# Ordering the last 48 rows of a sum of reciprocals by one list, in place of the last 24

## The chip, the cores and the metric

The kernel runs on one core of a Trainium2 chip. The metric is the device time of one execution in microseconds. The kernel before takes 169.41 us (median of the 6 runs that stood beside the changed kernel, 169.25 to 169.90). Ratios in this document are the mean time of one kernel's fast runs over the mean of the other's in the same rounds, so they are not quite the ratio of the medians quoted beside them.

## The reference

```python
x = np.abs(np.random.randn(32, 512, 1024)).astype(np.float32) + 1e-6
return np.sum(1.0 / x, axis=-1).astype(np.float32)
```

This is 67 MB in and 64 KB out. Each of the 128 partitions has 128 rows of 1024 numbers.

## The kernel before

A row has two halves, a and b. As 1/a + 1/b = (a + b) / (ab), half as many reciprocals are needed. GpSimd (or VectorE) makes the product ab, ScalarE makes 1/ab of it by Ln and Exp, and VectorE multiplies and sums. For some rows TensorE makes a + b in PSUM first (matmuls with an identity), and VectorE then has half the width to go over. Rows come into a ring of 40. Most rows are handled in a loop, in pairs. The last 24 follow a list, in which each letter is an operation and each number a row:

```python
    R = 40
    A, B, C = (2, 0, 0), (2, 2, 0), (2, 2, 1)
    LOADS = [[A, B, A, B], [A, B, A, C]] * 5 + [[A, B], [A, C]] * 3
    LAST = 104
    LAST_LOADS = [2] * 1 + [4] * 1 + [2] * 5 + [1] * 8
    ORDER = """
        P104 P105 L104+ P107 B106 E104+ V106 P109 B108 L106+ T104 P110+ S108
        ...
        S123 P124 E122+ T119 D125 S125 L124 T122 L125 P126 T121 E124 S126 E125
        T123 L126 T124 W127 E126 T125 X127 T126
    """
    # P product on GpSimd, D on VectorE; B copies b into PSUM for V, a product on VectorE;
    # S adds the halves on TensorE; L Ln, E Exp; T product and sum on VectorE;
    # W, X: Ln, and Exp with the sum, of a whole row. A plus sign: this row and the next.

    for n in LAST_LOADS:                       # all loads of the last rows, then the list
        xt = ring[:, c0 % R : c0 % R + n, :]
        keep(nc.sync.dma_start(out=xt, in_=x_v[:, c0 : c0 + n, :]))
        c0 += n
    ...
    nc.sync.dma_start(out=out_v, in_=sums)
```

All transfers are issued by SyncE, and their landings are counted in eight counters that take turns: transfer 1 uses the first, transfer 9 the first again. In the trace of the kernel before, each issue from the ninth load on comes after the landing of the load eight before, from the 19th load on 0.06 or 0.07 us after it. The kernel before has 31 loads and the output.

Of the kernel before, what the change touches and what calls it, by code (L numbers as in the profile page):

```python
# [11 lines left out]
def kernel(  # L12
# [15 lines left out]
    nc = tc.nc  # L28
# [4 lines left out]
    F = 128  # L33

    R = 40
# [3 lines left out]


    A, B, C = (2, 0, 0), (2, 2, 0), (2, 2, 1)
    LOADS = [[A, B, A, B], [A, B, A, C]] * 5 + [[A, B], [A, C]] * 3






    LAST = 104
    LAST_LOADS = [2] * 1 + [4] * 1 + [2] * 5 + [1] * 8  # L50
    ORDER = """
        P104 P105 L104+ P107 B106 E104+ V106 P109 B108 L106+ T104 P110+ S108
        E106+ V108 T105 L108+ S109 T106 L110+ P112+ T107 E108+ S112 E110 T108
        L112+ P114+ T109 S113 T110 E111 E112+ T111 L114+ P116 S116 T113 E114+
        T112 P117 L116 T114 P119 B118 L117 E116 S118 V118 E117 P120 T115 L118+
        P121 S119 T116 E118+ T117 P122 L120+ S122 T118 E120+ D123 L122+ T120
        S123 P124 E122+ T119 D125 S125 L124 T122 L125 P126 T121 E124 S126 E125
        T123 L126 T124 W127 E126 T125 X127 T126
    """

    Ln = mybir.ActivationFunctionType.Ln
# [4 lines left out]
    x_v = x.flatten_outer_dims().rearrange("(p f) d -> p f d", p=P)  # L66
# [24 lines left out]
    ring = opool.tile([P, R, D], f32)  # L91
# [3 lines left out]
    keep = tc.keep_in_program_order  # L95

    def add(bank, *halves):
        for k, half in enumerate(halves):
            i = nc.tensor.matmul(  # L99
                bank,  # L100
                lhsT=ident,
                rhs=half,
                start=k == 0,
                stop=k == len(halves) - 1,  # L104
            )
            keep(i)  # L106

    def sum_row(c, row, fac, out=None):
        i = nc.vector.tensor_tensor_reduce(  # L109
            out=row if out is None else out,  # L110
            in0=row,
            in1=fac,
            scale=S,
            scalar=0.0,
            op0=mult,
            op1=plus,
            accum_out=sums[:, c : c + 1],
        )
        keep(i)

    def sum_rows(c, xc, pr, sm, rc):
        m, e = xc.shape[1], len(sm)
        for j in range(e, m):
            row = xc[:, j, :].rearrange("p (h e) -> p h e", h=2)  # L124
            sum_row(  # L125
                c + j,  # L126
                row,
                rc[j - e].unsqueeze(1).to_broadcast([P, 2, H]),
                pr[:, e : e + 2, :] if j == e and e + 1 < m else None,
            )  # L130
        for j in reversed(range(e)):
            sum_row(c + j, pr[:, j, :], sm[j])

    waiting = None
    c0 = 0
    for chunks in LOADS:
        n = sum(m for m, _, _ in chunks)
        xt = ring[:, c0 % R : c0 % R + n, :]
# [3 lines left out]
        for m, e, v in chunks:  # L142
            pr = ppool.tile([P, m, H], f32, tag="ps" if e else "pr")
            for j in range(v):
# [3 lines left out]
                    out=pr[:, j, :], in0=xt[:, q + j, :H], in1=b, op=mult  # L148
# [6 lines left out]
        for (m, e, v), pr in zip(chunks, made):  # L155
            xc = xt[:, q : q + m, :]
            if v < m:
                i = nc.gpsimd.tensor_tensor(  # L158
                    out=pr[:, v:, :], in0=xc[:, v:, :H], in1=xc[:, v:, H:], op=mult
# [22 lines left out]
        c0 += n  # L182
    assert c0 == LAST, c0

    c0 = LAST
    for n in LAST_LOADS:
        xt = ring[:, c0 % R : c0 % R + n, :]
        keep(nc.sync.dma_start(out=xt, in_=x_v[:, c0 : c0 + n, :]))
        c0 += n
    assert c0 == F, c0  # L190
    sum_rows(*waiting)

    prs, rs, ss, bs = {}, {}, {}, {}
    order = ORDER.split()
# [3 lines left out]
    def pair(c):  # L198
        k = (c - LAST) // 2
        if k not in prs:  # L200
            pr = ppool.tile([P, 2, H], f32, tag=("pr", "ps")[k % 2])
            prs[k] = pr
        return prs[k]

    for op in order:
        kind, c, n = op[0], int(op[1:].rstrip("+")), 1 + op.endswith("+")
        j = (c - LAST) % 2
        rows = ring[:, c % R : c % R + n, :]
        a, b = rows[:, :, :H], rows[:, :, H:]
        pr = None if kind in "WX" else pair(c)[:, j : j + n, :]  # L210
        if kind == "P":
            keep(nc.gpsimd.tensor_tensor(out=pr, in0=a, in1=b, op=mult))  # L212
        elif kind == "D":
            keep(nc.vector.tensor_tensor(out=pr, in0=a, in1=b, op=mult))  # L214
        elif kind == "B":
            bb = bpool.tile([P, H], f32, tag="b")
            add(bb, b[:, 0, :])
            bs[c] = bb
        elif kind == "V":
            keep(  # L220
                nc.vector.tensor_tensor(  # L221
                    out=pr[:, 0, :], in0=a[:, 0, :], in1=bs[c], op=mult
                )
            )
        elif kind == "S":
            s = spool.tile([P, H], f32, tag="s")
            add(s, a[:, 0, :], b[:, 0, :])
            ss[c] = s
        elif kind == "L":
            keep(nc.scalar.activation(out=pr, in_=pr, func=Ln, scale=S))  # L230
        elif kind == "E":
            r = pr
            if c not in added:
                r = rpool.tile([P, n, H], f32, tag="rc")
                rs.update({c + l: r[:, l, :] for l in range(n)})
            keep(nc.scalar.activation(out=r, in_=pr, func=Exp, scale=-1.0))  # L236
            if n == 2:
                dead.add((c - LAST) // 2)
        elif kind == "T" and c in added:
            sum_row(c, pr[:, 0, :], ss[c])  # L240
        elif kind == "T":
            row = rows[:, 0, :].rearrange("p (h e) -> p h e", h=2)
            k = (c - LAST) // 2
            to = prs[k] if k in dead else None
            dead.discard(k)
            sum_row(c, row, rs[c].unsqueeze(1).to_broadcast([P, 2, H]), to)
        elif kind == "W":
            keep(nc.scalar.activation(out=rows, in_=rows, func=Ln))  # L248
        elif kind == "X":
            keep(  # L250
                nc.scalar.activation(
                    out=rows,
                    in_=rows,
                    func=Exp,
                    scale=-1.0,
                    accum_out=sums[:, c : c + 1],
                )
            )

    nc.sync.dma_start(out=out_v, in_=sums)  # L260

# [29 lines left out]
```

## Time and profile before

| Quantity | Before | View |
|---|---|---|
| traced span | 167.6 us | page |
| input queue, share of the span | 94.8% | DMA queues |
| row 127 lands | 161.8 us | issue and time to landing |
| ScalarE's last sum is read | 165.19 us | ScalarE's timeline |
| output issued, landed | 165.21, 166.8 us | the same views |

The table is read from the end: the stream of loads lasts until 161.8, the work on the last row 3.4 us more, then the output, and then some 0.8 us until the last instruction. The traced run took 169.71 us, 0.3 more than the median. The lines themselves stand in the prediction.

### The profile page before, as it was taken

How to read it: one execution, taken by the hardware profiler on the slowest of the kernel's cores; microseconds unless marked ns; L12 is line 12 of the kernel's file. 1: busy time of each engine (PE TensorE's matmuls, PEld its weight loads, DVE VectorE, ACT ScalarE, POOL GpSimd, SP SyncE). 2: the span in 40 equal slices, each digit the busy share in tenths (PEclk: the TensorE clock that was granted, in tenths of full speed). 3: DMA queues.
4: the chain of work that ended last, by engine and by line, in shares of the span. 5: the costliest groups of instructions: out<-in, count | busy, mean ns of one | idle time of the engine just before them, and what ended most of it. 6: DMA issues, size and time to landing. Idle time of an engine off the chain costs nothing.

```text
span 167.6 us, 1286 instructions
## 1 busy us (share of the span) xinstructions
PE 130.3 (78%) x274; PEld 50.2 (30%) x274; DVE 122.6 (73%) x267; ACT 134.8 (80%) x137; POOL 135.7 (81%) x73
## 2 busy tenths in 40 slices
PE   0007899796987959878699869977999995998990
PEld 0003343232233313322333224322343422433430
DVE  0000777758977578884788877778989899998994
ACT  3002888979789688868879788799999998999994
POOL 1007999699895999949998898999999997999630
PEclk9999999999999999999789999999999999999999
DMA  6999999999999999999999999999999999999910
GB/s 203 422 446 430 446 422 399 461 399 446 414 409 454 407 446 422 442 424 446 430 430 422 414 418 434 424 434 434 420 426 413 436 416 416 422 413 410 409 71 18
DMA packets 4615, 67.25 MB, mean 401 GB/s; under 512 B 512, under 2 KB 640, under 8 KB 1664
## 3 DMA queue, kind: packets, MB, share of 16 engines
q1 hardware_dynamic: 4608, 67.18, 94.8%
q8 instruction: 2, 0.03, 0.1%
q14 instruction: 5, 0.04, 0.1%
HBM read 67.11 MB, written 0.07 MB: 401 GB/s over the span
## 4 chain that ended last, share of the span: by engine, by line
DMA 72%; POOL 11%; ACT 9%; DVE 2%; issue 2%; PE 1%; ACTq 1%; SPq 0%; POOLq 0%
DMA ring<-in_x_dram 72%; POOL pr L158 11%; ACT pr L230 3%; ACT pr L169 2%; ACT pr L236 2%; DVE ring L109 1%; ACT r L236 1%; PE bb L99 1%; ACT r L174 1%; ACT ring L248 1%; ACTq L286 1%; DVE pr L109 0%; DVE pr L221 0%; SPq L139 0%; ACT pr L179 0%
## 5 line engine op out<-in xcount | busy, mean ns | idle before, releaser
L99 PE MATMUL s<-ring,ident 128*128 128x512 f32 x252 | 120.3, 617 | 30.7 <-DMA ring<-in_x_dram 15.2
L158 POOL TENSOR_TENSOR pr<-ring 128x1024 f32<-128x1024 f32 (+1 forms) x52 | 112.8, 2209 | 21.8 <-DMA ring<-in_x_dram 21.8
L99 PEld LDWEIGHTS s<-ring,ident 128*128 128x128 f32 x252 | 46.3, 193 | 101.8 <-issue 61.9
L169 ACT ACTIVATE pr<-pr 128x1024 f32<-128x1024 f32 x52 | 54.7, 1053 | 27.3 <-POOL pr L158 27.3
L109 DVE CUSTOM_DVE_ANT_1 pr<-ring,r 128x1024 f32<-128x1024 f32 x30 | 36.6, 1221 | 41.5 <-ACT r L174 40.8
L109 DVE CUSTOM_DVE_ANT_1 ring<-ring,r 128x1024 f32<-128x1024 f32 x34 | 41.3, 1217 | 0.0
L109 DVE CUSTOM_DVE_ANT_0 pr<-pr,s 128x512 f32<-128x512 f32 x63 | 40.9, 683 | 0.0
L179 ACT ACTIVATE pr<-pr 128x1024 f32<-128x1024 f32 x26 | 27.5, 1057 | 0.8
L174 ACT ACTIVATE r<-pr 128x1024 f32<-128x1024 f32 x26 | 26.7, 1028 | 0.8
L212 POOL TENSOR_TENSOR pr<-ring 128x512 f32<-128x512 f32 (+1 forms) x15 | 22.3, 1504 | 3.9 <-DMA ring<-in_x_dram 3.6
L230 ACT ACTIVATE pr<-pr 128x1024 f32<-128x1024 f32 (+1 forms) x14 | 12.5, 900 | 0.5 <-DVE pr L221 0.5
L109 DVE DVE_READ_ACCUMULATOR2_ANT sums<- 128x1 f32 x127 | 10.5, 83 | 0.0
L99 PE MATMUL b<-ring,ident 128*128 128x512 f32 x16 | 9.0, 646 | 0.3 <-DMA ring<-in_x_dram 0.2
L236 ACT ACTIVATE r<-pr 128x1024 f32<-128x1024 f32 (+1 forms) x8 | 6.4, 806 | 0.1
L236 ACT ACTIVATE pr<-pr 128x1024 f32<-128x1024 f32 (+1 forms) x7 | 6.0, 863 | 0.1
L147 DVE TENSOR_TENSOR pr<-ring,b 128x512 f32<-128x512 f32 x8 | 5.5, 684 | 0.7 <-PE b L99 0.7
L99 PE MATMUL bb<-ring,ident 128*128 128x512 f32 x6 | 3.4, 644 | 2.2 <-DMA ring<-in_x_dram 1.5
L99 PEld LDWEIGHTS b<-ring,ident 128*128 128x128 f32 x16 | 3.0, 207 | 6.0 <-DMA ring<-in_x_dram 4.1
L221 DVE TENSOR_TENSOR pr<-ring,bb 128x512 f32<-128x512 f32 x3 | 2.1, 688 | 0.4 <-PE bb L99 0.2
L99 PEld LDWEIGHTS bb<-ring,ident 128*128 128x128 f32 x6 | 0.9, 188 | 4.7 <-DMA ring<-in_x_dram 3.1
L70 ACT ACT_TABLE_LOAD x1 | 1.3, 1283 | 0.7 <-PEq L275 0.7
L214 DVE TENSOR_TENSOR pr<-ring 128x512 f32<-128x512 f32 x2 | 1.4, 686 | 0.0
(9 smaller groups left out, 3.2 us busy)
## 6 DMA issues: line engine op xcount, KB each, us to landing
ring<-in_x_dram SPq DMA_DIRECT2D x10, 4096.0 KB, 37.8
ring<-in_x_dram SPq DMA_DIRECT2D x7, 2048.0 KB, 37.0
ring<-in_x_dram SPq DMA_DIRECT2D x6, 1024.0 KB, 30.7
ring<-in_x_dram SPq DMA_DIRECT2D x8, 512.0 KB, 14.4
out_dram<-sums SPq DMA_DIRECT2D x1, 64.0 KB, 1.6
```

Of the source, the lines that this page charges most:

```text
L99: i = nc.tensor.matmul(bank, lhsT=ident, rhs=half, start=k == 0, stop=k == len(halves) - 1,)
L109: i = nc.vector.tensor_tensor_reduce(out=row if out is None else out, in0=row, in1=fac, scale=S, scalar=0.0, op0=mult, op1=plus, accum_out ...
L147: i = nc.vector.tensor_tensor(out=pr[:, j, :], in0=xt[:, q + j, :H], in1=b, op=mult)
L158: i = nc.gpsimd.tensor_tensor(out=pr[:, v:, :], in0=xc[:, v:, :H], in1=xc[:, v:, H:], op=mult)
L169: keep(nc.scalar.activation(out=pr, in_=pr, func=Ln, scale=S))
L174: nc.scalar.activation(out=r, in_=pr[:, e:, :], func=Exp, scale=-1.0)
L179: keep(nc.scalar.activation(out=r, in_=r, func=Exp, scale=-1.0))
L212: keep(nc.gpsimd.tensor_tensor(out=pr, in0=a, in1=b, op=mult))
L221: nc.vector.tensor_tensor(out=pr[:, 0, :], in0=a[:, 0, :], in1=bs[c], op=mult)
L230: keep(nc.scalar.activation(out=pr, in_=pr, func=Ln, scale=S))
L236: keep(nc.scalar.activation(out=r, in_=pr, func=Exp, scale=-1.0))
L248: keep(nc.scalar.activation(out=rows, in_=rows, func=Ln))
```

## The change

The intent is to order more of the end by hand, so that the last rows' products, Lns and sums come just in time. The list now covers rows 80 to 127. As the ring holds 40 rows, the loads of the last rows can't all be issued ahead of the list any more; each is placed in front of the first operation after which its place in the ring is free.

```diff
-    LOADS = [[A, B, A, B], [A, B, A, C]] * 5 + [[A, B], [A, C]] * 3
+    LOADS = [[A, B, A, B], [A, B, A, C]] * 5
-    LAST = 104
-    LAST_LOADS = [2] * 1 + [4] * 1 + [2] * 5 + [1] * 8
+    LAST = 80
+    LAST_LOADS = [4] * 7 + [2] * 4 + [1] * 12
     ORDER = """
-    (24 rows)
+        P80+ B82 S86 P83 L80+ S87 P84+ E80+ V82 L82+ T80 P86+ L84 T81 B90 E82+
+        ...
+        S123 T121 L124 E123 D125 E124 T122 S124 L125 W126 T123 D127 S127 E125
+        T124 L127 T125 E127 X126 T127
     """
...
+    def load(c0, below):
+        while LAST_LOADS and c0 + LAST_LOADS[0] - R <= below:
+            n = LAST_LOADS.pop(0)
+            ...
+        return c0
...
-    for op in order:
+    for at, op in enumerate(order):
+        c0 = load(c0, min(int(o[1:].rstrip("+")) for o in order[at:]))
```

It has 33 loads and the output, two more than before.

More of the change, by code (lines that the diff above doesn't have):

```diff
@@ L41 @@
     A, B, C = (2, 0, 0), (2, 2, 0), (2, 2, 1)
-    LOADS = [[A, B, A, B], [A, B, A, C]] * 5 + [[A, B], [A, C]] * 3
-    LAST = 104
-    LAST_LOADS = [2] * 1 + [4] * 1 + [2] * 5 + [1] * 8
+    LOADS = [[A, B, A, B], [A, B, A, C]] * 5
+    LAST = 80
+    LAST_LOADS = [4] * 7 + [2] * 4 + [1] * 12
     ORDER = """
-        P104 P105 L104+ P107 B106 E104+ V106 P109 B108 L106+ T104 P110+ S108
-        E106+ V108 T105 L108+ S109 T106 L110+ P112+ T107 E108+ S112 E110 T108
-        L112+ P114+ T109 S113 T110 E111 E112+ T111 L114+ P116 S116 T113 E114+
-        T112 P117 L116 T114 P119 B118 L117 E116 S118 V118 E117 P120 T115 L118+
-        P121 S119 T116 E118+ T117 P122 L120+ S122 T118 E120+ D123 L122+ T120
-        S123 P124 E122+ T119 D125 S125 L124 T122 L125 P126 T121 E124 S126 E125
-        T123 L126 T124 W127 E126 T125 X127 T126
+        P80+ B82 S86 P83 L80+ S87 P84+ E80+ V82 L82+ T80 P86+ L84 T81 B90 E82+
+        V90 L85 P88+ T82 L86+ B91 S90 T83 E86+ E85 V91 E84 T85 P92 L88+ T86
+        E88+ P93 T84 S91 L90+ P94+ T87 L92+ T88 S94 E90+ T89 P96+ E92+ T90
+        L94+ T91 S95 T93 P99 L96+ T92 S96 E94+ P98 E96 T94 E97 P101 B100 T95
+        L98+ S101 V100 P102+ L101 T97 E98+ S102 T96 L100 T98 L102+ T99 E100
+        P105 B104 E102 E101 S103 V104 P106+ E103 T101 L104+ T100 B108 E104+
+        T102 S106 P109 L106+ V108 T103 L108+ P110+ T104 S107 E106+ T105 E108+
+        S110 P112+ T106 L110+ T107 T108 S111 E110+ L112+ T109 P115 B114 E112+
+        T110 P116 S115 V114 T111 L114+ P117 T112 S114 E114+ P118 T113 L116+
+        S118 P119 T114 E116+ T115 P120 L118+ T117 S119 E118+ P121 T116 S120
+        L120 T119 P122 L121 T118 E120 S121 E121 D123 L122 T120 L123 D124 E122
+        S123 T121 L124 E123 D125 E124 T122 S124 L125 W126 T123 D127 S127 E125
+        T124 L127 T125 E127 X126 T127
     """
@@ L183 @@
     assert c0 == LAST, c0
-    c0 = LAST
-    for n in LAST_LOADS:
-        xt = ring[:, c0 % R : c0 % R + n, :]
-        keep(nc.sync.dma_start(out=xt, in_=x_v[:, c0 : c0 + n, :]))
-        c0 += n
-    assert c0 == F, c0
+    def load(c0, below):
+        while LAST_LOADS and c0 + LAST_LOADS[0] - R <= below:
+            n = LAST_LOADS.pop(0)
+            xt = ring[:, c0 % R : c0 % R + n, :]
+            keep(nc.sync.dma_start(out=xt, in_=x_v[:, c0 : c0 + n, :]))
+            c0 += n
+        return c0
     sum_rows(*waiting)
@@ L258 @@
             )
+    assert c0 == F, c0
     nc.sync.dma_start(out=out_v, in_=sums)
```

## The prediction

> **What bounds the kernel now.** I read the page's slices and queues first, then the rate in three stretches, then single loads from issue to landing, then ScalarE's timeline at the end. Of the page:
>
> ```profile
> DMA  6999999999999999999999999999999999999910
> ...
> q1 hardware_dynamic: 4608, 67.18, 94.8%
> ```
>
> The digits are DMA's busy tenths in 40 slices of the span: full in every slice but the first and the last two. One queue brings the 67.1 MB of input for 94.8% of the 167.6 us. So the kernel is a stream of loads with a short tail behind it, and only the stream's rate or the tail can be shortened. The rate by stretch (the last two columns are DMA share and GB/s; the stretches hold loads of four, two and one row):
>
> ```profile
> 102.40:131.90 29.50, 26.84 (x60) 10.71 (x60) 26.30 (x58) 27.71 (x28) 28.99 (x14) 1.00 1.01 427
> 139.30:151.70 12.40, 11.07 (x24) 4.30 (x24) 12.03 (x27) 11.92 (x14) 11.99 (x7) 1.00 1.01 419
> ```
>
> After the length come the busy us of PE, its weight loads, VectorE, ScalarE and GpSimd. All but the weight loads are 89 to 98% busy in both, yet the DMA share is 1.0: the engines keep pace and the stream never starves. The last load of one row, its issue in the timeline and its time to landing in the DMA view:
>
> ```profile
> 151.76 0.33 SPq L188 DMA_DIRECT2D ring<-in_x_dram  x1
> ```
>
> ```profile
> ring<-in_x_dram SPq DMA_DIRECT2D x1, 512.0 KB, 10.1
> ```
>
> Row 127 lands at 151.76 + 10.1 = 161.86. Read the same way, the last load of eight rows lands at 64.81 + 37.6 = 102.41, the sixth of four at 94.84 + 37.0 = 131.84, the two-row loads from 139.28 (104.48 + 34.8) to 151.73 (127.03 + 24.7). This gives 29.43 / 6 = 4.91 us for four rows, 12.45 / 5 = 2.49 for two, and 10.13 / 8 = 1.27 for one. The last issue, 151.76, comes just after a landing at 151.73, that of the load eight before it, as most late issues do; no row of the ring holds it.
>
> ScalarE towards that landing (a row's halves a and b are multiplied, ScalarE makes 1/ab of it by Ln and Exp, VectorE multiplies this with a + b and sums; PE adds the halves of some rows, and the last row of all is inverted whole, by ScalarE alone):
>
> ```profile
> 153.68 1.06 ACT L230 ACTIVATE pr<-pr 128x1024 f32<-128x1024 f32 x1 [0.15 <-DVE pr L221]
> 154.77 1.06 ACT L236 ACTIVATE pr<-pr 128x1024 f32<-128x1024 f32 x1
> 155.73 1.05 ACT L230 ACTIVATE pr<-pr 128x1024 f32<-128x1024 f32 x1
> ...
> 159.83 1.24 ACT L230 ACTIVATE pr<-pr 128x512 f32<-128x512 f32 x2
> 160.97 0.58 ACT L236 ACTIVATE r<-pr 128x512 f32<-128x512 f32 x1
> 161.49 0.61 ACT L236 ACTIVATE pr<-pr 128x512 f32<-128x512 f32 x1
> 162.05 0.63 ACT L230 ACTIVATE pr<-pr 128x512 f32<-128x512 f32 x1
> 162.59 1.04 ACT L248 ACTIVATE ring<-ring 128x1024 f32<-128x1024 f32 x1
> 163.53 0.61 ACT L236 ACTIVATE pr<-pr 128x512 f32<-128x512 f32 x1
> 164.05 1.04 ACT L251 ACTIVATE ring<-ring 128x1024 f32<-128x1024 f32 x1
> 165.00 0.19 ACT L251 ACTIVATION_READ_ACCUMULATOR ring<-ring 128x1 f32 x1
> ```
>
> From the Ln of rows 118 and 119 at 153.68 it never idles until 165.19, when the last row's sum is read and the output goes out; 2.4 us later the span ends. The whole-row Ln of row 127 (L248) starts 0.7 us after its data: ScalarE's backlog, not the landing, sets the end, but by less than 1 us.
>
> [...] Half-megabyte loads here, queued behind one another, cost 1.27 us a row against 4.91 / 4 = 1.23: only 3% less[...]. [...] two half-row Lns of 624 ns against one pair of 1052 differ by 196 ns.
>
> **The change part by part.**
>
> *Loads.* The 48 rows came in six loads of four, one of two, one of four, five of two, eight of one; now seven of four, four of two, twelve of one. From 102.41: 7 x 4.91 brings row 107 at 136.78, 4 x 2.49 row 115 at 146.74, 12 x 1.27 row 127 at 162.0. That is 0.1 us later than 161.86, the price of four more rows alone. Rows 116 to 119 come a little earlier one by one: row 119 at about 151.8 as before, 118 at 150.55.
>
> *When loads are issued.* They are now placed inside the list, each only after the work on the row 40 places before it. Row 127 needs row 87. By the rates below rows 80 to 87, landed at 112.2, are summed by about 126, and the rule of eight loads in flight allows the last issue only at about 151.9. There are some 25 us of slack, so the stream goes on unbroken.
>
> *Work by engine, last 48 rows.* Counted in both lists (the loop's 24 rows included): GpSimd loses two pair products of 2.38 and gains one single of 1.29, -3.5 us. VectorE gains two products from the ring and one from PSUM, 3 x 0.6 = +1.8 in start-to-start steps. PE gains one copy of a half, 0.86. ScalarE trades three pair Lns for six single and four pair Exps for eight single: seven times 0.15 to 0.2 us of overhead, +1.0 to 1.4. No engine was behind the stream by much, and each had waits in those 60 us, so all of this lies beside the loads except what falls into the last 10 us.
>
> *The tail.* In the listing above a pair's Ln to its own Exp takes 1.09 us start to start, a pair's Exp 0.96, a single Ln 0.57, a single Exp 0.52 into PSUM or 0.56 in place, the whole-row Ln 0.94, the last Exp with its read 1.14. Before, from 153.68: 3 x 2.05 + 3 x 0.57 + 0.52 + 0.56 + 0.52 + 0.94 + 1.14 = 11.54, against 11.51 seen. After, from the Ln of 118 and 119: 2.05 + seven single Lns 3.99 + five Exps in place 2.80 + two into PSUM 1.04 + 0.08 because the Exp of 127 follows its own Ln at once + 0.94 + 1.14 = 12.04. Splitting the pairs 120/121 and 122/123 costs this half microsecond. The start comes earlier: row 118's product starts at 150.6 on GpSimd, 119's ends at 150.6 + 2 x 1.29 = 153.2, where before 118 went over PE and VectorE to 153.6; ScalarE should be done with rows 116/117 at 153.4. So 153.4 + 12.0 = 165.4 to 165.5, against 165.19.
>
> *The floor under it.* Row 127 now goes by VectorE's product: 162.0 + 0.05 + 0.69 + 0.03, then Ln 0.65, Exp 0.56 and row 126's last Exp 1.14, to 165.1. The backlog still ends last, by about 0.3.
>
> Sum: +0.2 to +0.3 at the end of ScalarE's work, the output as before. I take +0.2: 169.43 + 0.2 = 169.6 us.
>
> **Rivals.**
>
> *A faster tail.* Half-width work on row 127 in place of a whole-row Ln could drain the backlog. Speaking for it is the 0.7 us in which row 127 waits for ScalarE; against it the sum above, and the floor of 165.1, which leaves 0.1 us: 169.3. Even a tail that ended with the last landing would save only 165.19 - 161.86 = 3.3 us, 2.0%.
>
> *The stream starves.* A load stuck behind a late sum or product would leave DMA idle, and each idle us would add itself to the time. The slack of 25 us speaks against it. A hole of 2 us would make 171.6.
>
> *The in-order queues trip over the new order.* PE has three buffers for sums and one for copies, and the Exps of rows not added on PE two; a list that asks for one too early holds the whole engine. Before, PE waits for VectorE in this way (5.2 us between 127 and 165) at no cost. If it happened late, in the last ten rows, 0.5 to 1 us would be lost: 170.1 to 170.4. The change orders the list over all 48 rows, so I expect no more of it than before.
>
> *Smaller loads cost more than seen*, 1.35 a row in place of 1.27: +1 us, 170.5. The eight single loads before show nothing of it.
>
> **Range and chances.** The two ends I can work out, floor and backlog, lie 0.3 us apart, and a mis-stepped buffer costs under 1 us: 169.2 to 170.2. Two per cent is 3.4 us; faster would need more than the whole tail, slower a hole in the stream. Faster 0.01, within 2% 0.97, slower 0.02.
>
> **What would show it right or wrong.** DMA at 9 in slices 2 to 38; row 127 landing at 161.9 to 162.1; the last issue at about 151.9; ScalarE without idle from about 153.4 to 165.4 and first among the pieces of the chain's end. Wrong would be: a gap in the DMA row, a landing after 162.5, a wait of ScalarE or VectorE of over 0.5 us in the last 10 us, or an end of ScalarE's work before 165.0.

Cut from it are general figures for the ceiling of the data rate, for the size of transfers and for the cost of a ScalarE operation, which no trace here shows. The forecast's sum rests on none of them: it is worked out from the times in its listings and stays 169.43 + 0.2 = 169.6 us. That no order of loads could win much in the stream rested on the ceiling alone; measured are 427 GB/s with a DMA share of 1.0. Its eight loads in flight are what the trace shows by the waits described under "The kernel before".

## The result

The changed kernel takes 169.95 us (median of 6, 169.63 to 170.06) against 169.41: ratio 1.0026, 95% interval 1.0011 to 1.0041. Executions over 1.5% slower than the fastest of the same kernel are left out of the means. That is the same within 2%, and inside the predicted range. Its page:

```profile
DMA  5999999999999999999999999999999999999900
...
q1 hardware_dynamic: 4896, 67.18, 94.2%
q14 instruction: 6, 0.05, 0.1%
```

The stream is as unbroken as before. The last of these lines counts fetches of instructions within the span: six packets of 8 KB each, one more than before. The one more starts at 168.02, 0.67 us after SyncE's 80th recorded instruction; SyncE has 79 in the kernel before, and there a fetch starts at 168.64, after the span. It matters later. The stretches of four-row and two-row loads:

```profile
102.40:131.90 29.50, 24.01 (x52) 9.24 (x53) 27.16 (x57) 27.61 (x31) 28.61 (x16) 1.00 1.01 428
139.30:146.70 7.40, 7.40 (x19) 3.33 (x19) 7.40 (x18) 7.33 (x9) 7.06 (x5) 1.00 1.01 414
```

The DMA share is 1.0 in both, at 428 GB/s in the first, as before. ScalarE's timeline at the end:

```profile
153.22 1.04 ACT L240 ACTIVATE pr<-pr 128x1024 f32<-128x1024 f32 x1
154.30 1.06 ACT L246 ACTIVATE pr<-pr 128x1024 f32<-128x1024 f32 x1
155.26 1.13 ACT L240 ACTIVATE pr<-pr 128x512 f32<-128x512 f32 x2
156.30 1.13 ACT L246 ACTIVATE pr<-pr 128x512 f32<-128x512 f32 x2
...
161.93 0.57 ACT L246 ACTIVATE r<-pr 128x512 f32<-128x512 f32 x1
162.71 0.63 ACT L240 ACTIVATE pr<-pr 128x512 f32<-128x512 f32 x1 [0.21 <-DVE pr L224]
...
164.85 0.19 ACT L261 ACTIVATION_READ_ACCUMULATOR ring<-ring 128x1 f32 x1
```

Two single Lns start 155.26, and what follows them starts 156.30: 0.52 us each. At 162.71 ScalarE waits 0.21 us for the product of row 127: it has no backlog left. It is done at 165.04, earlier than before. The chain of waits says the same (start, length, what):

```profile
151.78 10.10 DMA ring<-in_x_dram
...
161.98 0.70 DVE pr L224
...
162.71 0.64 ACT pr L240
...
163.37 0.63 ACT pr L246
```

Row 127's load, issued at 151.78, lands at 161.88; then its product, its Ln, its Exp. The landing sets the end, by the path that the prediction called the floor.

So the work ends 0.15 us earlier, and the output lands at 166.6 in place of 166.8, yet the span is 168.2 in place of 167.6. The loss lies after the output's landing. SyncE's instructions of the kernel's exit from that landing on, before and then after (count, shortest/median/longest in ns, first and last start; the count of three before includes the check that saw the landing, which stands outside the five after):

```profile
L286 SPq EVENT_SEMAPHORE  x3: 17/17/28, 166.8 to 167.5; - x3
L286 SPq DRAIN  x3: 7/7/7, 166.8 to 167.2; - x3
```

```profile
L297 SPq EVENT_SEMAPHORE  x5: 17/28/28, 166.7 to 168.1; - x5
L297 SPq DRAIN  x3: 7/7/129, 166.9 to 167.7; - x3
```

Three checks more follow the landing, and one of the drains, the second, takes 129 ns and not 7; it starts at 167.35, 0.42 us after the first, where before there are 0.06 between them. In parts, from the instruction records (us):

| | landing seen to first drain | to second drain | to the end of the span | sum |
|---|---|---|---|---|
| before | 0.07 | 0.06 | 0.69 | 0.82 |
| after | 0.27 | 0.42 | 0.82 | 1.51 |

The exit costs 0.69 us more. The prediction had it "as before".

### The profile page after: what moved, and what is told of

The parts are those of the page before. It is cut to its first block, busy times and chain, and to the rows that moved or that the text cites. A ratio compares the mean times of both kernels' runs of the same rounds, so it can differ in the third digit from the quotient of the medians.

```text
span 168.2 us, 1302 instructions
## 1 busy us (share of the span) xinstructions
PE 129.8 (77%) x276; PEld 50.2 (30%) x276; DVE 123.8 (74%) x270; ACT 134.4 (80%) x144; POOL 132.3 (79%) x72
## 4 chain that ended last, share of the span: by engine, by line
DMA 67%; ACT 10%; POOL 7%; PE 5%; issue 4%; DVE 4%; SPq 1%; ACTq 1%; POOLq 0%; DVEq 0%
DMA ring<-in_x_dram 67%; POOL pr L164 7%; PE s L105 4%; ACT pr L240 3%; ACT r L246 2%; ACT pr L175 2%; ACT pr L246 2%; SPq L145 1%; DVE ring L115 1%; DVE pr L115 1%; ACT r L180 1%; ACTq L297 1%; PE bb L105 1%; DVE pr L224 0%; DVE pr L231 0%
## 5 line engine op out<-in xcount | busy, mean ns | idle before, releaser
L164 POOL TENSOR_TENSOR pr<-ring 128x1024 f32<-128x1024 f32 (+1 forms) x40 | 88.0, 2232 | 21.7 <-DMA ring<-in_x_dram 21.7
L175 ACT ACTIVATE pr<-pr 128x1024 f32<-128x1024 f32 x40 | 42.2, 1055 | 27.1 <-POOL pr L164 27.1
L222 POOL TENSOR_TENSOR pr<-ring 128x512 f32<-128x512 f32 (+1 forms) x26 | 43.6, 1702 | 2.4 <-DMA ring<-in_x_dram 1.3
L240 ACT ACTIVATE pr<-pr 128x1024 f32<-128x1024 f32 (+1 forms) x29 | 25.0, 883 | 1.2 <-DVE pr L231 0.7
L185 ACT ACTIVATE pr<-pr 128x1024 f32<-128x1024 f32 x20 | 21.2, 1058 | 0.6
L180 ACT ACTIVATE r<-pr 128x1024 f32<-128x1024 f32 x20 | 20.6, 1028 | 0.6
L246 ACT ACTIVATE r<-pr 128x1024 f32<-128x1024 f32 (+1 forms) x15 | 12.6, 843 | 0.2
L246 ACT ACTIVATE pr<-pr 128x512 f32<-128x512 f32 (+1 forms) x16 | 12.4, 805 | 0.2
L105 PE MATMUL bb<-ring,ident 128*128 128x512 f32 x14 | 7.4, 610 | 1.1 <-DVE pr L231 0.9
L105 PE MATMUL b<-ring,ident 128*128 128x512 f32 x10 | 5.6, 645 | 0.1
L231 DVE TENSOR_TENSOR pr<-ring,bb 128x512 f32<-128x512 f32 x7 | 4.8, 684 | 0.5 <-PE bb L105 0.5
```

The source lines that it names most:

```text
L105: i = nc.tensor.matmul(bank, lhsT=ident, rhs=half, start=k == 0, stop=k == len(halves) - 1,)
L164: i = nc.gpsimd.tensor_tensor(out=pr[:, v:, :], in0=xc[:, v:, :H], in1=xc[:, v:, H:], op=mult)
L175: keep(nc.scalar.activation(out=pr, in_=pr, func=Ln, scale=S))
L180: nc.scalar.activation(out=r, in_=pr[:, e:, :], func=Exp, scale=-1.0)
L185: keep(nc.scalar.activation(out=r, in_=r, func=Exp, scale=-1.0))
L222: keep(nc.gpsimd.tensor_tensor(out=pr, in0=a, in1=b, op=mult))
```

## The experiments

My first theory was the **place** of the output's counter. At the exit SyncE checks the eight counters in five instructions, in the same order in both traces. The output is transfer 32 before, whose counter is in the fifth check, and transfer 34 after, whose counter is in the second: three checks are left over for after the landing. The rivals were the **length** of SyncE's program (83 recorded instructions against 79) and the **tail** on ScalarE, as predicted. Tiny loads of 32 bytes, put between the eight-row loads, move the output to another counter and add nothing to the stream:

```diff
+    TINY = {9: [1], 8: [0]}                    # b_t2; six or eight entries in the others
...
+        for t in TINY.get(c0 // 8, []):        # after the loads that begin at rows 32 to 72
+            keep(nc.sync.dma_start(out=spare[:, 8*t : 8*t+8],
+                                   in_=x_v[0:1, 0, 8*t : 8*t+8]))
```

**Before, with two tiny loads** (b_t2).

> The kernel before with two loads of 32 bytes added in mid-stream, so that the output is the 34th transfer, as in the changed kernel; list and load sizes as before. Theory 1 (place): SyncE's last checks go over the eight landing counters in a fixed order, the output's counter now stands second in it and not last, so the time from the output's landing to the end of the span grows from 0.84 us to about 1.5; 169.4 becomes 170.0, ratio 1.0035. Theory 2 (length): the exit grows because SyncE's program is longer; two transfers more give the same 1.5 and 170.0. Theory 3 (the prediction's): the list's tail on ScalarE is what costs; this kernel has the list of before, so exit 0.84 and 169.4, ratio 1.000.

170.13 us, ratio 1.0029 (1.0005 to 1.0054). With the list of before, the exit is that of the changed kernel: 1.51 us from the landing seen to the end, with one drain of 121 ns. So the exit comes from the two transfers more and not from the list. The tail theory falls for this part; place and length are still both possible.

**Before, with eight tiny loads** (b_t8).

> The kernel before with eight such loads, so the output is the 40th transfer and its counter is again the last one checked. Place: exit 0.84, 169.4, ratio 1.000. Length: SyncE's program is now longer than the changed kernel's, so exit 1.5 or more, 170.0, ratio 1.0035. The prediction's: 169.4.

170.52 us, ratio 1.0043 (1.0015 to 1.0071): the time that length had predicted, but not in its place. From the landing seen to the end it took 0.82, as place had said. The output, however, was issued at 165.50 though ScalarE's last sum had been read at 165.11, and SyncE waited longer for its landing:

```profile
SPq L295 <- DMA out_dram<-sums: 1.5, 1, 1.5
```

against 0.9 in the kernel before. A fetch of instructions ran at 166.14, while the output was under way; that it held up the output is not shown. (The exit here is short, and yet the time long: the stall, from 165.11 to 165.50, now stands before the output's issue.)

**Changed kernel, with six tiny loads** (a_t6).

> The changed kernel with six such loads, so its output too is the 40th transfer and its counter the last one checked. Place: exit 0.84 in place of 1.54, ScalarE's work still ends at about 165.05, so 169.3 and ratio 0.999, faster than both. Length: exit 1.5, 169.95, ratio 1.003. The prediction's: the tail is the list's, nothing changes, 169.95.

169.28 us, ratio 0.9991 (0.9955 to 1.0027), and a span of 167.3 in place of 168.2. The exit is 0.82, as place expected and length did not. But this trace has a stall too, where it does no harm. SyncE's instructions for the last load:

```profile
L205 SPq EVENT_SEMAPHORE  x1: 17/17/17, 151.6 to 151.6; - x1
L205 SPq DMA_DIRECT2D ring<-in_x_dram x1: 328/328/328, 152.0 to 152.0; - x1
```

The check passes at 151.58 and the issue starts at 152.02, 0.44 us later; such a pair is usually 0.06 apart.

**The changed kernel again** (a_again).

> The changed kernel once more, on the same chip and in the same rounds: does the exit of 1.54 us come again, and with it 169.95 (ratio 1.003)? If the exit varies from run to run (0.84 to 1.54), no theory of its cause by program is needed: then 169.3 to 170.

170.26 us, ratio 1.0036 (1.0010 to 1.0063); the exit was 1.51 again, with the stall at the same instruction. So in both runs it stands at the same place of the program. The times of one kernel scatter here more than in the first rounds, from 169.55 to 170.70.

Counting SyncE's recorded instructions gives the second theory. In all the four programs with more than 79 of them the stall comes just after the **79th**: in the exit (83 instructions, changed kernel and b_t2), before the output's issue (90, b_t8), before the last load's issue (92, a_t6). The kernel before has exactly 79. I call this place a **boundary** of the program; what happens in the hardware there is not shown. Drains on SyncE, in a stretch where it has nothing to do (3.7 to 25.0 us in the kernel before), move the program across it and leave the counters alone:

```diff
+        if c0 == 32:                           # after the fifth load is issued
+            for _ in range(4):                 # or 16
+                keep(nc.sync.drain())
```

**Before, with four drains** (b_d4).

> The kernel before with four empty instructions (drains) on SyncE after its fifth load, where SyncE has 20 us to spare. In every trace so far SyncE lost some 0.4 us right after its 79th recorded instruction: in the changed kernel (83) inside the exit, in the run with eight tiny loads before the output's issue, in the one with six in mid-stream; the kernel before has 79 in all. Boundary theory: now 83 instructions, the output's counter still checked last, so the exit grows by the boundary's part alone, 0.36 before the second drain and 0.12 after it, from 0.82 to 1.3 us; 169.4 becomes 169.9, ratio 1.003. Place alone: exit 0.82, 169.4, ratio 1.000.

170.06 us, ratio 1.0031 (1.0009 to 1.0052). The exit takes 1.31 us: 0.08 to the first drain, 0.43 to the second, 0.80 to the end.

```profile
L289 SPq DRAIN  x3: 7/7/116, 167.2 to 168.0; - x3
```

The slow drain is there with the counter in its old place: the boundary's part by itself is 1.31 - 0.82 = 0.49. (In this traced run ScalarE also ended 0.4 us late, at 165.57; why, I did not find.)

**Before, with sixteen drains** (b_d16).

> The same with sixteen: SyncE has 95, its 79th falls in mid-stream, just after the issue of the load of row 125, where loads are issued 10 us ahead. Boundary: the stall is hidden, exit 0.82, ratio 1.000, though the program is longer than in any slower kernel. A cost that simply grows with length: 170 or more.

169.75 us, ratio 1.0006 (0.9986 to 1.0025). The exit is 0.82 and all its drains take 7 ns, with 95 recorded instructions. Length as such cost nothing here; where the boundary falls did, 0.49 us in b_d4.

The DMA records show a companion of the boundary. In every traced run with an 80th recorded instruction on SyncE, one fetch of 8 KB starts after that instruction, 0.6 to 0.9 us later at the end of the kernel (168.02 in the changed kernel) and 1.7 to 3.3 us later in mid-stream (150.82 here). The kernel before has no 80th; there it starts at 168.64, 1.04 us after the end of the span. The time less the span is 2.11 to 2.12 us in the means of the runs of b_d16 and of the kernel before alike, so what stands after the span costs nothing that shows.

**Changed kernel, with sixteen drains** (a_d16).

> The changed kernel with the sixteen drains: the boundary in mid-stream, the output's counter still second of the eight, so place alone: three checks after the landing, exit 0.82 + 0.21 = 1.03; ScalarE ends 0.14 earlier than before; 169.5, ratio 1.0004. If the boundary were the whole of it: exit 0.82, 169.3. If place were the whole: exit 1.5, 170.0.

169.20 us, ratio 0.9978 (0.9960 to 0.9996), 0.3 us below what place had said. The exit takes 0.98: 0.22 to the first drain, 0.06 to the second, 0.70 to the end.

```profile
L300 SPq EVENT_SEMAPHORE  x5: 17/28/28, 166.5 to 167.3; - x5
L300 SPq DRAIN  x3: 7/7/7, 166.6 to 166.9; - x3
```

The three checks after the landing are still there, the slow drain is not. So place is worth 0.98 - 0.82 = 0.16 us and the boundary 0.49; the two together, 0.65, are close to the 0.69 of the changed kernel.

**Changed kernel, six tiny loads, once more** (a_t6_again).

> The changed kernel with six tiny loads once more, beside b_d16, which has the list of before and an exit of the same 0.82 us: the difference of the two is what the list and its loads are worth by themselves. From the traces so far 0.14 to 0.3 us, so 169.1 to 169.3 and ratio 0.999 or 0.998; it should beat both kernels.

168.94 us, ratio 0.9965 (0.9943 to 0.9987): it beats the kernel before, and the changed one. Against b_d16, with the same exit, it is 0.8 us faster by the medians, where the traced spans, 167.2 against 167.6, differ by 0.4. More than I expected.

The rest of that difference is outside the trace. The time less the traced span is 1.77 to 1.81 us in all five traced runs of the changed list and 1.99 to 2.14 in those of the old one. In the kernel before, the fetch at SyncE's boundary starts 1.04 us after the traced end; that another engine has a boundary there which costs time was my guess. Four kernels, each the one before with sixteen drains on one engine at its start, test this (in the trace of the kernel before ScalarE is idle from 2.0 to 15.8 us):

```diff
+    for _ in range(16):
+        keep(nc.scalar.drain())                # or vector, gpsimd, tensor
```

> A rest is open: the measured time less the traced span is 2.11 us in kernels with the list of before, 1.77 to 1.81 in those with the changed list, 0.3 us that no span shows. Theory: another engine meets such a boundary of its program after the traced end in the kernel before, and not in the changed one. Sixteen drains on ScalarE, at the start[...], move its boundaries by sixteen instructions: if ScalarE is the engine, time less span falls to 1.8. If not, 2.11. Rival: the rest has to do with what the list does to data or power, then none of the four runs changes it.

> The same on VectorE. Time less span 1.8 if VectorE is the engine (it has 324 recorded instructions before and 331 after the change), else 2.11.

> The same on GpSimd (133 before, 126 after the change). Time less span 1.8 if GpSimd is the engine, else 2.11.

> The same on TensorE (567 before, 577 after the change). Time less span 1.8 if TensorE is the engine, else 2.11.

These are single runs of unknown state; what is read is the difference of time and span within a run:

| drains on | time | traced span | difference |
|---|---|---|---|
| ScalarE | 169.21 | 167.44 | 1.77 |
| VectorE | 169.37 | 167.27 | 2.10 |
| GpSimd | 169.40 | 167.26 | 2.14 |
| TensorE | 169.50 | 167.37 | 2.13 |

Of the four engines it is ScalarE: sixteen instructions more on it give the difference of the changed kernel, 1.77, on the others it stays at 2.10 to 2.14. How the changed list comes to the same difference is not shown. In b_act16 fetches start at 59.90 and 162.96 us, after ScalarE's 64th and 192nd recorded instruction; in the kernel before and in the changed one a fetch starts at 74.63 and 74.62, after its 64th there too. They have 183 and 185 of these instructions, so neither trace reaches a 192nd, and what happens after the traced end is not shown. The kernels b_t2 and b_t8, with 182, have a difference of about 1.94 in the mean of their runs, and that is not explained either.

## Why the prediction was right, and where it was not

The time was right, 169.95 for 169.6 with 169.2 to 170.2, and "within 2%" with it. That it is "within 2%" follows from what bounds the kernel, and this was read rightly. That it is slower by a few tenths, as forecast, is luck: the +0.2 came from a tail that turned out shorter, and the measured +0.4 from an exit that the prediction had taken as unchanged.

*What bounds the kernel.* Right: the stream is whole (DMA share 1.0) and sets all but the last microseconds: row 127 lands at 161.88 in a span of 168.2.

*Loads.* Row 127 was to land at 162.0 and landed at 161.88. The last issue was to come at about 151.9 and came at 151.78. Over the traced runs in which its landing can be read the row lands at 161.66 on average in the kernel before and its variants (eight runs) and 161.67 in the changed one and its variants (five), so the 0.1 us for four more single rows is too small to be seen. Queued behind one another, loads of 512 KB cost 1.27 us a row in the kernel before and loads of 2 MiB 1.23.

*The tail.* This is the term of the wrong sign. The step that failed is "a single Ln 0.57, a single Exp 0.52 into PSUM or 0.56 in place". They take 0.52 each, as the timeline after shows. The two single Lns that I had read it from took 1.24 us because the second of them had to wait for its product on VectorE, which ended only at 160.41, 0.58 after the first Ln had started; the gap was too short for the view to name it. Two single Exps, 1.04, against a pair, 0.96, differ by 0.08; I had charged 0.15 to 0.2. Seven Lns 0.05 too long and five Exps 0.04 are 0.55 us of the 12.04. Seen are 165.04 - 153.22 = 11.82, of which 0.26 lie between what the Exp at 161.93 should have taken and the Ln at 162.71, so 11.56 of work. The backlog that was to end "last, by about 0.3" is gone, and the floor holds: landing to ScalarE's end 3.15 us, where the prediction's own floor is 165.1 - 162.0 = 3.1. In all five traced runs of the changed list this stretch is 3.14 or 3.15; with the old list it is 3.35 to 3.39 in six runs of eight (3.14 and 3.95 in the other two). The list with its loads gains 0.22 us there in place of losing 0.2 to 0.3.

*The output.* "The output as before" is the other step that failed: +0.69 in the exit, 0.49 from the boundary on SyncE and 0.16 from the place of the output's counter, both made by the two loads more and not by the order of rows.

*Outside the span*, where the prediction had nothing: -0.34. Sixteen drains on ScalarE make the same difference in the kernel before (1.77 in b_act16); how the list makes it is not shown.

The three make -0.22 + 0.69 - 0.34 = +0.1 us, and measured are +0.4 (the ratio's) in the first rounds and +0.6 in the second. The rest, 0.3 to 0.5 us, stays open. The parts come from traced runs, one for each kernel and round, while timed runs of one kernel differ by up to 1 us. But the record has a span for every run of the experiments and of the changed kernel. By these the time less the span is 1.76 to 1.80 us in the means of the changed list's five sets of runs and 2.11 to 2.12 in those of the kernel before, so the -0.34 holds, and the open rest lies inside the span: in the second rounds the mean span is 168.40 against 167.54, 0.86 more, where the parts give -0.22 + 0.69 = 0.47. In the third rounds, with the two changed kernels whose exit was mended, the parts fit: mean spans of 167.45 (a_d16) and 167.25 (a_t6_again) against 167.47, so -0.02 and -0.22, where the parts give -0.22 + 0.16 = -0.06 and -0.22.

*The rivals.* "A faster tail" was nearer to the truth than I gave it: 0.2 us were there. The stream did not starve. PE waited 2.0 us for VectorE between 155 and 166 us, but none of it is in the chain that ended last. The single-row loads land 1.22 to 1.29 us apart in both traces, save one step of 1.41 after the change.

## What to carry to other kernels

When a change moves a time by less than a microsecond, follow the trace to its very last instruction: what happened here after the output had landed, 0.69 us, weighed more than the tail that the change was made for, 0.22. The number of transfers (0.16) and of instructions on the issuing engine (0.49) made nearly all of it, so compare a hand-made order with one in which these are the same. And a step read from two instructions in a row may hold a wait that is too short to be named, as the two Lns of 1.24 us did, which take 1.13 where nothing is waited for; take it from a place where nothing can be waited for.
